# Pre-norm weights applied before the transposes in a hybrid attention block

## The chip, the cores and the metric

The kernel runs on one core of one Trainium2 chip. The metric is the device time of one execution in microseconds; the time shown is the median of three runs, and a further execution was profiled.

## The reference

One layer of a decoder block: x (512 rows of 1024, f32) is RMS-normalised, projected by w_in (1024 x 5912) to the inputs of two attention branches, their gates and their merge gates; the branches are projected, merged, projected by w_o, normalised again and added to x. What the change touches is the first step and the first use of it:

```python
def rms_norm(x, g):
    xf = x.astype(jnp.float32)
    y = xf * lax.rsqrt(jnp.mean(xf * xf, axis=-1, keepdims=True) + RMS_EPS)
    return (y * g.astype(jnp.float32)).astype(x.dtype)
...
    u = rms_norm(x, norm_pre)
    proj = u @ w_in
    q_a, kv_a, g_a, z_a, qkv_b, z_b, merge = jnp.split(proj, splits, axis=-1)
```

## The kernel before, in words

Every product has to be near f32, so an operand is split into a rounded part (hi, type f32r) and the rest (lo), and a product is the sum of hi x hi, lo x hi and hi x lo. The normalised input u is needed transposed (its 1024 columns on the partitions, in eight pieces k, the 512 rows free) and split: the tiles uh and ul, which nearly all that follows reads.

The program has a prologue, then a long stream. The **prologue** (lines 509 to 729) makes uh and ul and, meanwhile, a small projection: 280 columns (values of two NSA branches and the head gates, weights ra, split into wa_hl). The rows come in four tiles tt of 128. For each tile, before:

- x_stats (L554): ACT squares the tile and sums over the row (sq, ss); Vector scales the sum (L514, L564, L565); POOL raises it to -1/2 (L515, L566), which gives rs, one factor a row.
- x_transpose (L581): TensorE, eight blocks of 128 columns, in two halves h. For tiles 0 and 1 the right operand is the diagonal matrix of rs (x_diag, L575), a full f32 product (L588), which scales and transposes at once. For tiles 2 and 3 ACT scales the tile first (x_scale, L579), and the transpose uses the identity (L590).
- x_hi (L593): Vector multiplies the transposed half by the norm_pre weight of each partition (npreT, L596) out of PSUM into SBUF, and ACT rounds it into uh (L600). x_low: the difference goes to ul (L604), on Vector or, for two halves, on POOL.
- a_mm (L618): the small projection, in three parts of eight products: uh by hi weights, ul by hi, uh by lo (parts 0, 1, 2; L626). a_evac_act and a_evac_dve bring the result (pa) into v_slc, v_win and gates.

wa_hi and wa_lo split the small weights, two pieces k a call (ACT L610, POOL L608; lo on Vector or POOL, L613). `first` holds the eight pieces in which the weights of kcvc, the first chunk of the stream, are split (ACT L118, Vector L119). keep_warm (L650) issues products whose result nobody reads. The x and ra loads and the weight loads are all issued on SP's queue, in program order.

What sets the order in the prologue is the program text: inside `with tc.manual_schedule()` each engine's queue takes its instructions in the order in which the lines issue them, and each waits only for its inputs. The exception on POOL are the memsets of rowsel and klos, which are written behind the prologue (L746 to L752) and stand early in POOL's queue all the same; klos is the zero-padded lower part of the keys, first written by the chunk after kcvc.

The **stream** then runs chunk by chunk: each projects uh and ul by a slice of w_in in 512-column products (L171 to L173), while the next chunk's weights are split, and attention units and the merge follow. kcvc's products need all of uh and ul.

Of the kernel before, what the change touches and what calls it, by code (L numbers as in the profile page):

```python
# [41 lines left out]
def hybrid_block(ctx, tc, x, norm_pre, w_in, pe_k, w1_k, w2_k, pe_v, w1_v, w2_v,  # L42
# [469 lines left out]
    def rstd_of(ss, r, eps):  # L512

        dve.tensor_scalar(r, ss, 1.0 / D, eps, op0=ALU.mult, op1=ALU.add)  # L514
        pool.tensor_tensor(r, r, neghalf, op=ALU.pow)  # L515

    warm = const.tile([128, 1], F32, name="warm")
    act.activation(warm, neghalf, AF.Exp)
    xt = [early.tile([128, D], F32, name=f"x_{tt}") for tt in range(NT)]
    npre = early.tile([KT, 128], F32, name="npre")  # L520
    npreT = early.tile([128, KT], F32, name="npreT")
# [15 lines left out]
    nc.sync.dma_start(npre, norm_pre.rearrange("(k p) -> k p", k=KT))  # L537
# [14 lines left out]
    rs, up, sss = {}, {}, {}  # L552

    def x_stats(tt, parts=1):  # L554
        sq = s4.tile([128, D], F32, tag="s4", name=f"sq_{tt}")
        ss = early.tile([128, 2], F32, name=f"ss_{tt}")
        rs[tt] = early.tile([128, 1], F32, name=f"rs_{tt}")
        w = D // parts
        for n in range(parts):
            act.activation(sq[:, n * w:n * w + w], xt[tt][:, n * w:n * w + w], AF.Square, accum_out=ss[:, n:n + 1])  # L560
        sss[tt] = ss
        if parts == 2:
            r = rs[tt]
            dve.tensor_scalar(ss[:, 0:1], ss[:, 0:1], 1.0 / D, EPS, op0=ALU.mult, op1=ALU.add)  # L564
            dve.scalar_tensor_tensor(r, ss[:, 1:2], 1.0 / D, ss[:, 0:1], op0=ALU.mult, op1=ALU.add)  # L565
            pool.tensor_tensor(r, r, neghalf, op=ALU.pow)  # L566

    def x_stats_r(tt):
        rstd_of(sss[tt][:, 0:1], rs[tt], EPS)

    diag = {}

    def x_diag(tt):
        diag[tt] = early.tile([128, 128], F32, name=f"diag_{tt}")
        dve.tensor_scalar(diag[tt], ident, rs[tt], None, op0=ALU.mult)  # L575

    def x_scale(tt, h):
        c = slice(512 * h, 512 * h + 512)
        act.activation(xt[tt][:, c], xt[tt][:, c], AF.Copy, scale=rs[tt])  # L579

    def x_transpose(tt, h):  # L581

        pt = ps("to"[h], f"ut_{tt}_{h}")
        for k in range(4):
            kk = 4 * h + k
            o, i = pt[:, k * 128:(k + 1) * 128], xt[tt][:, kk * 128:(kk + 1) * 128]
            if tt in diag:
                mm(o, i, diag[tt], start=True, stop=True)  # L588
            else:
                pe_eng.transpose(o, i, ident)  # L590
        up[tt, h] = pt

    def x_hi(tt, h):  # L593

# [547 lines left out]
```

## Time and profile before

| | |
|---|---|
| median of the runs shown | 471.07 us (470.97 to 471.8, three runs) |
| the profiled execution | 471.45 us |
| its span, first to last instruction | 469.7 us |
| TensorE (PE) busy | 459.0 us, 98% of the span |
| Vector (DVE) busy | 326.4 us, 69% |
| ACT busy | 255.8 us, 54% |
| POOL (GpSimd) busy | 125.8 us, 27% |
| DMA | 42.08 MB, mean 90 GB/s; 275 GB/s in the first 11.7 us |

Times in the profile count from the first instruction of the span. An engine's busy time says little about what ends last: for that the chain of waits is followed back from the end, and the stretch in question is read instruction by instruction. PE is TensorE's products and PEld its weight loads; a row "x32" merges that many instructions in a row, and "us" of a merged row goes from its start to its end. A full f32 product shows as two rows of PE. A PE row's own duration holds the pipeline; what a stream costs is the spacing of starts.

### The profile page before, as it was taken

What the parts mean: (1) busy time and instruction counts of PE and PEld (TensorE: products, weight loads), DVE (VectorE), ACT (ScalarE), POOL (GpSimd) and SP (SyncE); (2) the same over time, 40 slices, a digit from 0 to 9 for tenths busy, and PEclk for the clock granted to TensorE, in tenths of its full rate; (3) what the DMA queues carried; (4) which work ended last, traced back from release to release, by engine and by line L of the source; (5) the groups of instructions that cost most, each with busy time, mean ns of one, the idle gap of its engine ahead of it and who ended that gap; (6) DMA issues with size and microseconds to landing.
All of it is one profiled execution on the core that took longest, in us unless ns stands there. A gap on an engine that the chain in (4) does not pass through costs nothing.

```text
span 469.7 us, 6991 instructions
## 1 busy us (share of the span) xinstructions
PE 459.0 (98%) x2408; PEld 388.1 (83%) x2408; DVE 326.4 (69%) x837; ACT 255.8 (54%) x684; POOL 125.8 (27%) x144
## 2 busy tenths in 40 slices
PE   7999999999999999999999999999999999999994
PEld 6988887888999888788888888887888888888884
DVE  3858868998777878877798978777674264265044
ACT  5754657776566758656675866675433333234021
POOL 6600006433231333323144443432221010020000
PEclk9999999999999999999999999999999999999998
DMA  8657125023032031130220222132135324224133
GB/s 275 191 161 199 45 51 174 2 77 104 7 84 91 1 91 46 45 89 15 77 91 14 76 89 54 38 92 71 64 93 138 109 63 137 89 89 135 45 134 136
DMA packets 45091, 42.08 MB, mean 90 GB/s; under 512 B 1624, under 2 KB 39808, under 8 KB 45056
## 3 DMA queue, kind: packets, MB, share of 16 engines
q1 hardware_dynamic: 44912, 41.12, 29.4%
q10 hardware_dynamic: 144, 0.52, 0.3%
q8 instruction: 19, 0.31, 0.3%
q14 instruction: 16, 0.13, 0.1%
HBM read 39.54 MB, written 2.10 MB: 89 GB/s over the span
## 4 chain that ended last, share of the span: by engine, by line
PE 88%; DVE 6%; ACT 3%; POOL 1%; issue 1%; POOLq 0%; DVEq 0%; ACTq 0%
PE t L976 5%; PE mm_ga L171 3%; PE mm_ga L172 3%; PE mm_ga L173 3%; PE mm_gb L172 3%; PE mm_gb L173 3%; PE mm_gb L171 3%; PE s L937 3%; PE s L938 3%; PE o L997 3%; PE o L996 3%; PE pa L626 2%; PE mm_qkb L172 2%; PE mm_qkb L173 2%; PE mm_qkb L171 2%; PE mm_vb L290 2%
## 5 line engine op out<-in xcount | busy, mean ns | idle before, releaser
L943 ACT ACTIVATE p<-p,st 128x512 f32<-128x512 f32 (+3 forms) x96 | 53.1, 555 | 23.5 <-DVE st L941 23.2
L955 POOL TENSOR_SCALAR p<-p,st 128x256 f32<-128x256 f32 (+1 forms) x48 | 44.1, 929 | 64.6 <-DVE st L952 22.9
L977 ACT ACTIVATE pt<-t 128x512 fp32r<-128x512 f32 (+1 forms) x72 | 35.4, 524 | 27.4 <-PE t L976 26.8
L978 DVE TENSOR_TENSOR pt<-t,pt 128x512 fp32r<-128x512 f32 (+1 forms) x72 | 40.8, 594 | 8.1 <-ACT pt L977 7.7
L941 DVE CUSTOM_DVE_ANT_0 p<-s,bias_a 128x512 f32<-128x512 f32 (+3 forms) x64 | 29.1, 484 | 10.5 <-PE s L938 10.4
L976 PE MATMUL t<-ident,p 128*128 128x128 f32 x240 | 34.7, 274 | 1.3 <-DVE pt L978 1.0
L976 PEld LDWEIGHTS t<-ident,p 128*128 128x128 f32 x240 | 27.5, 140 | 6.1 <-DVE pt L978 3.3
L354 POOL TENSOR_TENSOR ga<-ga,gb 128x512 f32<-128x512 f32 x8 | 11.7, 1464 | 77.2 <-DVE gb L353 77.2
L1004 POOL TENSOR_TENSOR z<-ot,z 64x512 f32<-64x512 f32 x16 | 20.6, 1285 | 21.8 <-DVE ot L1003 21.8
L171 PE MATMUL mm_qkb<-uh,ws_qkb 128*128 128x512 f32 x64 | 25.8, 404 | 0.0
L171 PE MATMUL mm_gb<-uh,ws_gb 128*128 128x512 f32 x64 | 25.6, 400 | 0.0
L171 PE MATMUL mm_ga<-uh,ws_ga 128*128 128x512 f32 x64 | 25.6, 400 | 0.0
L955 DVE TENSOR_SCALAR p<-p,st 128x512 f32<-128x512 f32 (+1 forms) x48 | 25.2, 564 | 0.5
L172 PE MATMUL mm_gb<-ul,ws_gb 128*128 128x512 f32 x64 | 25.4, 396 | 0.0
L173 PE MATMUL mm_gb<-uh,ws_gb 128*128 128x512 f32 x64 | 25.3, 396 | 0.0
L172 PE MATMUL mm_qkb<-ul,ws_qkb 128*128 128x512 f32 x64 | 25.3, 395 | 0.0
L172 PE MATMUL mm_ga<-ul,ws_ga 128*128 128x512 f32 x64 | 25.3, 395 | 0.0
L173 PE MATMUL mm_ga<-uh,ws_ga 128*128 128x512 f32 x64 | 25.3, 395 | 0.0
L173 PE MATMUL mm_qkb<-uh,ws_qkb 128*128 128x512 f32 x64 | 25.2, 394 | 0.0
L119 DVE TENSOR_TENSOR ws_ab<-raw_ab,ws_ab 128x256 fp32r<-128x256 f32 x32 | 12.8, 455 | 16.7 <-ACT ws_ab L118 16.7
L895 POOL TENSOR_SCALAR bias_a<-dbase 128x512 f32<-128x512 f32 x8 | 13.2, 1650 | 37.8 <-DVE st L941 33.0
L895 POOL TENSOR_SCALAR bias_b<-dbase 128x512 f32<-128x512 f32 x8 | 12.3, 1543 | 38.2 <-DVE st L941 38.2
(312 smaller groups left out, 1388.9 us busy)
## 6 DMA issues: line engine op xcount, KB each, us to landing
raw_qkb<-in_w_in_dram SPq DMA_DIRECT2D x8, 512.0 KB, 5.2
raw_ga<-in_w_in_dram SPq DMA_DIRECT2D x4, 1024.0 KB, 5.1
raw_gb<-in_w_in_dram SPq DMA_DIRECT2D x4, 1024.0 KB, 5.1
raw_wo<-in_w_o_dram SPq DMA_DIRECT2D x4, 1024.0 KB, 5.0
raw_qa<-in_w_in_dram SPq DMA_DIRECT2D x4, 512.0 KB, 6.4
raw_za<-in_w_in_dram SPq DMA_DIRECT2D x4, 512.0 KB, 5.2
raw_vb<-in_w_in_dram SPq DMA_DIRECT2D x2, 1024.0 KB, 5.3
raw_zb<-in_w_in_dram SPq DMA_DIRECT2D x2, 1024.0 KB, 5.6
```

Of the source, the lines that this page charges most:

```text
L171: mm(dst, v[:, 0, k], rh(n), start=(n == 0), stop=False)
L172: mm(dst, v[:, 0, k], rl(n), start=False, stop=False)
L173: mm(dst, v[:, 1, k], rh(n), start=False, stop=(n == len(kts) - 1))
L895: pool.tensor_scalar(t, dbase, slope, None, op0=ALU.mult)
L937: mm(sp[:, 0:nn], q, hi, start=True, stop=False)
L941: dve.tensor_tensor_reduce(pp, src, bias[:, 384 - 128 * i:512], 1.0, 3.0e38, ALU.add, ALU.min, st[:, 0, i:i + 1])
L943: act.activation(pp, pp, AF.Exp, bias=st[:, 0, i:i + 1], scale=-1.0, accum_out=st[:, 1, i:i + 1])
L955: (dve if i >= 2 else pool).tensor_scalar(pp, pp, st[:, 1, i:i + 1], None, op0=ALU.mult)
L976: pe_eng.transpose(tp[:, b * 128:(b + 1) * 128], p_of(u, i)[:, 128 * j:128 * j + 128], ident)
L977: act.activation(h[:, c0:c0 + n], tp[:, 0:n], AF.Copy)
L978: dve.tensor_tensor(l[:, c0:c0 + n], tp[:, 0:n], f(h[:, c0:c0 + n]), op=ALU.subtract)
L1004: pool.tensor_tensor(zs[zt][mine], t[mine], zs[zt][mine], op=ALU.mult)
```

## The change

norm_pre is no longer transposed into one weight a partition. It is loaded as one row (by ACT's queue), and two products with a row of ones (L649) spread it over all 128 partitions into two PSUM tiles npb, one a half. x_scale (L568) multiplies each half tile of x on Vector by rs and by npb in one instruction, in place, for all four tiles; all transposes are then plain ones by the identity (L574); x_hi (L581) rounds straight out of PSUM on ACT, and x_low (L585) reads PSUM too, always on Vector. The 13 warm-ups become 3 ahead of the spreading products and 6 behind them. wa_hi(2) goes to POOL beside wa_hi(4), all wa_lo to Vector. The memsets of rowsel and klos become `clear()`, called near the end of the prologue. The rest of the order is written anew.

```diff
@@ -509,16 +509,13 @@
     early_cm = tc.tile_pool(name="early", bufs=1)
     early = early_cm.__enter__()
 
-    def rstd_of(ss, r, eps):
-
-        dve.tensor_scalar(r, ss, 1.0 / D, eps, op0=ALU.mult, op1=ALU.add)
-        pool.tensor_tensor(r, r, neghalf, op=ALU.pow)
-
     warm = const.tile([128, 1], F32, name="warm")
+    npre = early.tile([1, D], F32, name="npre")
+    nc.scalar.dma_start(npre, norm_pre[None, :])
+    ones = early.tile([1, 128], F32, name="ones")
+    dve.memset(ones, 1.0)
     act.activation(warm, neghalf, AF.Exp)
     xt = [early.tile([128, D], F32, name=f"x_{tt}") for tt in range(NT)]
-    npre = early.tile([KT, 128], F32, name="npre")
-    npreT = early.tile([128, KT], F32, name="npreT")
     ra = early.tile([128, KT, 280], F32, name="ra")
     wa_hl = early.tile([128, 2, KT, 280], F32R, name="wa_hl")
     gates = const.tile([128, NT, 24], F32, name="gates")
@@ -534,7 +531,6 @@
         nc.sync.dma_start(ra[:, k, 128:280], cols(C_VW, 152)[:, k])
 
     load_x(0, 2)
-    nc.sync.dma_start(npre, norm_pre.rearrange("(k p) -> k p", k=KT))
     load_x(1)
     load_ra(0)
     load_ra(1)
@@ -549,59 +545,44 @@
         for i in range(2 if kv == "k" else 1):
             nc.sync.dma_start(t[:, 128 + 64 * i:192 + 64 * i], w2[kv])
 
-    rs, up, sss = {}, {}, {}
+    rs, ut = {}, {}
 
     def x_stats(tt, parts=1):
+
         sq = s4.tile([128, D], F32, tag="s4", name=f"sq_{tt}")
         ss = early.tile([128, 2], F32, name=f"ss_{tt}")
-        rs[tt] = early.tile([128, 1], F32, name=f"rs_{tt}")
+        r = rs[tt] = early.tile([128, 1], F32, name=f"rs_{tt}")
         w = D // parts
         for n in range(parts):
             act.activation(sq[:, n * w:n * w + w], xt[tt][:, n * w:n * w + w], AF.Square, accum_out=ss[:, n:n + 1])
-        sss[tt] = ss
+        part = EPS
         if parts == 2:
-            r = rs[tt]
-            dve.tensor_scalar(ss[:, 0:1], ss[:, 0:1], 1.0 / D, EPS, op0=ALU.mult, op1=ALU.add)
-            dve.scalar_tensor_tensor(r, ss[:, 1:2], 1.0 / D, ss[:, 0:1], op0=ALU.mult, op1=ALU.add)
-            pool.tensor_tensor(r, r, neghalf, op=ALU.pow)
-
-    def x_stats_r(tt):
-        rstd_of(sss[tt][:, 0:1], rs[tt], EPS)
-
-    diag = {}
-
-    def x_diag(tt):
-        diag[tt] = early.tile([128, 128], F32, name=f"diag_{tt}")
-        dve.tensor_scalar(diag[tt], ident, rs[tt], None, op0=ALU.mult)
+            part = ss[:, 0:1]
+            dve.tensor_scalar(part, part, 1.0 / D, EPS, op0=ALU.mult, op1=ALU.add)
+        dve.tensor_scalar(r, ss[:, parts - 1:parts], 1.0 / D, part, op0=ALU.mult, op1=ALU.add)
+        pool.tensor_tensor(r, r, neghalf, op=ALU.pow)
 
     def x_scale(tt, h):
+
         c = slice(512 * h, 512 * h + 512)
-        act.activation(xt[tt][:, c], xt[tt][:, c], AF.Copy, scale=rs[tt])
+        dve.scalar_tensor_tensor(xt[tt][:, c], xt[tt][:, c], rs[tt], npb[h], op0=ALU.mult, op1=ALU.mult)
 
     def x_transpose(tt, h):
-
         pt = ps("to"[h], f"ut_{tt}_{h}")
         for k in range(4):
             kk = 4 * h + k
-            o, i = pt[:, k * 128:(k + 1) * 128], xt[tt][:, kk * 128:(kk + 1) * 128]
-            if tt in diag:
-                mm(o, i, diag[tt], start=True, stop=True)
-            else:
-                pe_eng.transpose(o, i, ident)
-        up[tt, h] = pt
+            pe_eng.transpose(pt[:, k * 128:(k + 1) * 128], xt[tt][:, kk * 128:(kk + 1) * 128], ident)
+        u = pt.rearrange("p (k t) -> p k t", k=4)
+        a = slice(tt * 128, tt * 128 + 128)
+        ut[tt, h] = u, uh[:, 4 * h:4 * h + 4, a], ul[:, 4 * h:4 * h + 4, a]
 
     def x_hi(tt, h):
-
-        u = xt[tt][:, 512 * h:512 * h + 512].rearrange("p (k t) -> p k t", k=4)
-        dve.tensor_tensor(u, up[tt, h].rearrange("p (k t) -> p k t", k=4),
-                          npreT[:, 4 * h:4 * h + 4, None].to_broadcast([128, 4, 128]), op=ALU.mult)
-        hi = uh[:, 4 * h:4 * h + 4, tt * 128:tt * 128 + 128]
-        up[tt, h] = (u, hi)
+        u, hi, lo = ut[tt, h]
         act.activation(hi, u, AF.Copy)
 
-    def x_low(tt, h, eng=dve):
-        u, hi = up[tt, h]
-        eng.tensor_tensor(ul[:, 4 * h:4 * h + 4, tt * 128:tt * 128 + 128], u, f(hi), op=ALU.subtract)
+    def x_low(tt, h):
+        u, hi, lo = ut[tt, h]
+        dve.tensor_tensor(lo, u, f(hi), op=ALU.subtract)
 
     def wa_hi(k, eng=None):
         if eng is not None:
@@ -611,6 +592,16 @@
 
     def wa_lo(k, eng=dve):
         eng.tensor_tensor(wa_hl[:, 1, k:k + 2], ra[:, k:k + 2], f(wa_hl[:, 0, k:k + 2]), op=ALU.subtract)
+
+    def clear():
+
+        pool.memset(rowsel, 0.0)
+        for i in range(4):
+            pool.memset(rowsel[32 * i:32 * i + 32, i % 2:i % 2 + 1], 1.0)
+        for t in klos:
+            for n in range(2):
+                pool.memset(f(t[64:128, n, 0]), 0.0)
+                pool.memset(f(t[0:64, n, 1]), 0.0)
 
     vst["slc"], vst["win"] = s4tile("v_slc"), s4tile("v_win")
     apt = {}
@@ -643,89 +634,97 @@
 
     first = [p for sl in range(2) for p in take_pieces(order[sl])]
     both = (0, 1)
-    wt = ps("mm", "warmup")
+    wt = ps("s", "warmup")
 
     def keep_warm(n):
         for _ in range(n):
             mm(wt, warmup[:, 0:128], warmup[:, 0:512], start=True, stop=True)
 
     with tc.manual_schedule():
-        keep_warm(13)
+        lo, hi = range(0, 4), range(4, 8)
+        keep_warm(3)
+
+        npb = [ps("mm", f"npre_{h}") for h in range(2)]
+        for h in range(2):
+            mm(npb[h], ones, npre[:, 512 * h:512 * h + 512], start=True, stop=True)
+        wt = ps("s", "warmup2")
+        keep_warm(6)
         x_stats(0, 2)
-        pt = ps("t", "npreT_ps")
-        pe_eng.transpose(pt[:, 0:KT], npre, ident[0:KT, 0:KT])
+        x_scale(0, 0)
+        x_transpose(0, 0)
+        x_scale(0, 1)
+        x_hi(0, 0)
+        x_transpose(0, 1)
+        x_low(0, 0)
         x_stats(1)
-        x_diag(0)
-        x_transpose(0, 0)
-        x_stats_r(1)
-        dve.tensor_copy(npreT, pt[:, 0:KT])
+        wa_hi(2, pool)
         wa_hi(0)
-        x_transpose(0, 1)
-        x_diag(1)
+        x_hi(0, 1)
+        a_mm(0, (0,), 2, lo)
+        x_scale(1, 0)
+        a_mm(0, (1,), 2, lo)
+        x_scale(1, 1)
+        x_low(0, 1)
+        wa_hi(4, pool)
         x_transpose(1, 0)
-        wa_hi(2)
-        x_hi(0, 0)
-        wa_hi(4, pool)
         wa_hi(6)
-        wa_lo(4, pool)
         x_transpose(1, 1)
-        x_hi(0, 1)
+        x_hi(1, 0)
+        wa_lo(0)
+        x_hi(1, 1)
+        wa_lo(2)
+        a_mm(0, (0, 1), 2, hi)
         x_stats(2)
-        a_mm(0, (0,))
-        x_hi(1, 0)
-        x_low(0, 0)
-        x_low(0, 1)
-        x_hi(1, 1)
-        x_stats_r(2)
-        a_mm(0, (1,))
-        wa_lo(0)
+        x_low(1, 0)
+        a_mm(0, (2,), 2, lo)
+        x_low(1, 1)
+        a_mm(1, (0,), 2, lo)
+        a_mm(1, (0,), 2, hi)
+        wa_lo(4)
+        a_mm(1, (1,), 2, lo)
+        wa_lo(6)
+        a_mm(1, (1,), 2, hi)
+        x_scale(2, 0)
+        a_mm(1, (2,), 2, lo)
+        x_scale(2, 1)
+        a_mm(0, (2,), 2, hi)
         x_stats(3)
-        a_mm(1, (0,))
-        a_mm(0, (2,), 2, (4, 5, 0, 1))
-        x_scale(2, 0)
-        x_scale(2, 1)
-        wa_lo(2)
-        x_stats_r(3)
-        a_mm(1, (2,), 2, (4, 5, 0, 1))
+        a_evac_act(0)
+        a_mm(1, (2,), 2, hi)
         x_transpose(2, 0)
-        wa_lo(6)
-        x_scale(3, 1)
-        a_mm(0, (2,), 2, (2, 3, 6, 7))
-        x_low(1, 1, pool)
-        x_low(1, 0)
-        x_scale(3, 0)
+        a_evac_dve(0)
         x_transpose(2, 1)
         x_hi(2, 0)
-        a_evac_act(0)
-        a_mm(1, (2,), 1, (2, 3, 6, 7))
+        a_evac_act(1)
+        x_hi(2, 1)
+        a_evac_dve(1)
+        x_low(2, 0)
+        x_scale(3, 0)
+        a_mm(2, (0,), 2, lo)
+        x_scale(3, 1)
+        x_low(2, 1)
+        a_mm(2, (0,), 2, hi)
+        a_mm(2, (2,), 1)
+        x_transpose(3, 0)
         x_transpose(3, 1)
-        x_hi(2, 1)
-        x_low(2, 0)
-        x_low(2, 1, pool)
-        x_transpose(3, 0)
-        a_evac_dve(0)
-        a_mm(1, (1,), 1)
         x_hi(3, 0)
         x_hi(3, 1)
-        a_evac_act(1)
-        a_mm(2, (0,))
+        a_mm(2, (1,), 1)
         x_low(3, 0)
-        a_mm(2, (2,), 1)
-        a_mm(2, (1,), 1)
-        a_evac_dve(1)
+        a_evac_act(2)
         x_low(3, 1)
         first[0]()
-        a_evac_act(2)
         first[1]()
+        a_evac_dve(2)
         first[2]()
         first[3]()
         first[4]()
+        a_mm(3, (0, 2, 1), 1)
         first[5]()
-        a_mm(3, (0, 1, 2))
         first[6]()
+        clear()
         a_evac_act(3)
         a_evac_dve(3)
-        a_evac_dve(2)
         first[7]()
 
     early_cm.__exit__(None, None, None)
@@ -743,13 +742,6 @@
     pool.memset(f(kcs), 0.0)
     pool.memset(f(kcl), 0.0)
     vcs = const.tile([128, 2, 2, 128], F32R, name="vcs")
-    pool.memset(rowsel, 0.0)
-    for i in range(4):
-        pool.memset(rowsel[32 * i:32 * i + 32, i % 2:i % 2 + 1], 1.0)
-    for t in klos:
-        for n in range(2):
-            pool.memset(f(t[64:128, n, 0]), 0.0)
-            pool.memset(f(t[0:64, n, 1]), 0.0)
     blk, pe2, w2t = {}, {}, {}
     for kv in "kv":
         t = cvt[kv]
```

How the queues stand around the first tiles. TensorE, from its start; before:

```order
L650 MATMUL warmup_128<-warmup_79 128x512 x13
L656 MATMUL npreT_ps_152<-ident_78,npre_99 128x8
L588 MATMUL ut_0_0_160<-diag_0_158,x_0_95 128x128 x4
L588 MATMUL ut_0_1_169<-diag_0_158,x_0_95 128x128 x4
L588 MATMUL ut_1_0_176<-diag_1_174,x_1_96 128x128 x4
L588 MATMUL ut_1_1_187<-diag_1_174,x_1_96 128x128 x4
L626 MATMUL pa_0_198<-wa_hl_102,uh_76 128x280 x8
L626 MATMUL pa_0_198<-wa_hl_102,ul_77 128x280 x8
```

and now (warmup, npre and ut are PSUM tiles, ut_0_1 is tile 0, half 1):

```order
L641 MATMUL warmup_129<-warmup_79 128x512 x3
L649 MATMUL npre_0_135<-npre_94,ones_96 128x512
L649 MATMUL npre_1_136<-npre_94,ones_96 128x512
L641 MATMUL warmup2_139<-warmup_79 128x512 x6
L574 MATMUL ut_0_0_155<-ident_78,x_0_99 128x128 x4
L574 MATMUL ut_0_1_162<-ident_78,x_0_99 128x128 x4
L617 MATMUL pa_0_177<-wa_hl_104,uh_76 128x280 x4
L617 MATMUL pa_0_177<-wa_hl_104,ul_77 128x280 x4
L574 MATMUL ut_1_0_190<-ident_78,x_1_100 128x128 x4
L574 MATMUL ut_1_1_196<-ident_78,x_1_100 128x128 x4
L617 MATMUL pa_0_177<-wa_hl_104,uh_76 128x280 x4
```

The diagonal products and npre's transpose are gone; two products from npre stand between the warm-ups, and tile 0's first small products (pa_0) now come ahead of tile 1's transposes.

ACT, from its first square; before:

```order
L560 ACTIVATE sq_0_144,ss_0_145<-x_0_95 128x512 x2
L560 ACTIVATE sq_1_154,ss_1_155<-x_1_96 128x1024
L610 ACTIVATE wa_hl_102<-ra_101 128x560 x2
L600 ACTIVATE uh_76<-x_0_95 128x4x128
L610 ACTIVATE wa_hl_102<-ra_101 128x560
L600 ACTIVATE uh_76<-x_0_95 128x4x128
L560 ACTIVATE sq_2_194,ss_2_195<-x_2_97 128x1024
L600 ACTIVATE uh_76<-x_1_96 128x4x128 x2
```

and now, from the start of its queue:

```order
L514 DMA npre_94<-in_norm_pre_dram 1x1024
L517 ACT_TABLE_LOAD
L517 ACTIVATE warm_93<-neghalf_85 128x1
L557 ACTIVATE sq_0_146,ss_0_147<-x_0_99 128x512 x2
L581 ACTIVATE uh_76<-ut_0_0_155 128x4x128
L557 ACTIVATE sq_1_168,ss_1_169<-x_1_100 128x1024
L591 ACTIVATE wa_hl_104<-ra_103 128x560
L581 ACTIVATE uh_76<-ut_0_1_162 128x4x128
L591 ACTIVATE wa_hl_104<-ra_103 128x560
L581 ACTIVATE uh_76<-ut_1_0_190 128x4x128
L581 ACTIVATE uh_76<-ut_1_1_196 128x4x128
L557 ACTIVATE sq_2_213,ss_2_214<-x_2_101 128x1024
```

x_hi(0,0), the first uh row, moved ahead of tile 1's square; wa_hi's calls on ra stand between x_hi's; tile 2's squares follow both halves of tile 1; the scales of x_2 and x_3 are gone.

Vector, around tile 2's row sum (rs_2 from ss_2); before:

```order
L604 TENSOR_TENSOR ul_77<-x_0_95,uh_76 128x4x128 x2
L596 TENSOR_TENSOR x_1_96<-ut_1_1_187,npreT_100 128x512
L514 TENSOR_SCALAR rs_2_196<-ss_2_195 128x1
L613 TENSOR_TENSOR wa_hl_102<-ra_101,wa_hl_102 128x560 x2
L514 TENSOR_SCALAR rs_3_226<-ss_3_225 128x1
L613 TENSOR_TENSOR wa_hl_102<-ra_101,wa_hl_102 128x560
L604 TENSOR_TENSOR ul_77<-x_1_96,uh_76 128x4x128
L596 TENSOR_TENSOR x_2_97<-ut_2_0_250,npreT_100 128x512
```

and now:

```order
L568 SCALAR_TENSOR_TENSOR x_1_100<-x_1_100,rs_1_170,npre_0_135 128x512
L568 SCALAR_TENSOR_TENSOR x_1_100<-x_1_100,rs_1_170,npre_1_136 128x512
L585 TENSOR_TENSOR ul_77<-ut_0_1_162,uh_76 128x4x128
L594 TENSOR_TENSOR wa_hl_104<-ra_103,wa_hl_104 128x560 x2
L562 TENSOR_SCALAR rs_2_215<-ss_2_214 128x1
L585 TENSOR_TENSOR ul_77<-ut_1_0_190,uh_76 128x4x128
L585 TENSOR_TENSOR ul_77<-ut_1_1_196,uh_76 128x4x128
L594 TENSOR_TENSOR wa_hl_104<-ra_103,wa_hl_104 128x560 x2
L568 SCALAR_TENSOR_TENSOR x_2_101<-x_2_101,rs_2_215,npre_0_135 128x512
L568 SCALAR_TENSOR_TENSOR x_2_101<-x_2_101,rs_2_215,npre_1_136 128x512
```

The sum stood behind all of Vector's work on tile 1 but x_low(1,0), with two wa_lo and tile 3's sum next. Now tile 2's sum stands ahead of x_low for both halves of tile 1 and of the last two wa_lo.

## Rows read from the trace of the kernel before

**Rows 1.** Spans and granted clock of the cores.
```profile
core 0: 469.7 us, clock 0.996
```

**Rows 2.** Stretches (length; busy and count of PE, PEld, DVE, ACT, POOL; clock, DMA, GB/s).
```profile
7.20:10.80 3.60, 3.56 (x32) 3.57 (x32) 2.36 (x6) 2.35 (x6) 0.71 (x2) 1.00 1.10 361
10.80:13.70 2.90, 2.08 (x16) 1.65 (x14) 2.90 (x4) 2.66 (x5) 2.21 (x2) 1.00 1.04 369
13.70:27.00 13.30, 13.30 (x103) 12.86 (x103) 11.43 (x27) 10.80 (x31) 6.21 (x10) 1.00 0.44 116
27.00:470.00 443.00, 435.08 (x2249) 366.43 (x2248) 308.60 (x800) 236.42 (x639) 110.97 (x111) 0.99 0.28 83
```

**Rows 3.** Waits of TensorE from 27 us on (us in total, times, longest).
```profile
PE t L976 <- DVE pt L978: 1.0, 2, 0.6
```

**Rows 4.** Chain of waits, 0 to 28 us (start us, us, what).
```profile
5.82 0.52 POOL klos L752
6.34 0.53 POOL rs L566
...
6.89 0.30 DVE diag L575
...
7.24 2.96 PE ut L588 x24
...
18.74 0.87 PE ut L590 x8
19.61 7.21 PE pa L626 x56
...
27.48 0.23 PE mm_kcvc L172
```

**Rows 5.** Stretches, the warm-up line L650 alone (first: PE busy and count).
```profile
1.50:4.50 3.00, 3.00 (x7) 2.42 (x8) 1.00 0.81 261
```

**Rows 6.** Instructions in order of time, 0 to 7 us.
```profile
0.72 0.86 SPq L529 DMA_DIRECT2D x<-in_x_dram  x2
...
3.45 0.63 ACT L560 ACTIVATE sq<-x 128x512 f32<-128x512 f32 x1 [1.24 <-DMA x<-in_x_dram]
...
4.85 0.16 DVE L565 SCALAR_TENSOR_TENSOR rs<-ss 128x1 f32<-128x1 f32 x1 [0.49 <-ACT sq L560]
...
6.46 1.06 ACT L560 ACTIVATE sq<-x 128x1024 f32<-128x1024 f32 x1 [1.64 <-DMA x<-in_x_dram]
```

**Rows 7.** The tile npost: ACT issue of its load, time to landing.
```profile
L1064 ACTq DMA_DIRECT2D npost<-in_norm_post_dram x1: 379/379/379, 330.3 to 330.3; - x1
...
DMA to landing us min/median/max: 3.7/3.7/3.7
```

**Rows 8.** Groups by line and form, 0 to 27 us.
```profile
L119 DVE TENSOR_TENSOR ws_kcvc<-raw_kcvc,ws_kcvc 128x256 fp32r<-128x256 f32 x7 | 2.5, 418 | 0.7 <-ACT ws_kcvc L118 0.7
...
L751 POOL MEMSET klos<- 64x512 f32 x4 | 2.1, 521 | 0.2
...
L610 ACT ACTIVATE wa_hl<-ra 128x560 fp32r<-128x560 f32 x3 | 1.9, 665 | 1.3 <-DMA ra<-in_w_in_dram 1.3
...
L608 POOL CAST wa_hl<-ra 128x560 fp32r<-128x560 f32 x1 | 0.7, 650 | 2.2 <-DMA ra<-in_w_in_dram 2.2
...
L566 POOL TENSOR_TENSOR rs<-rs,neghalf 128x1 f32<-128x1 f32 x1 | 0.5, 549 | 0.0
```

**Rows 9.** Groups by line and form, whole span.
```profile
L977 ACT ACTIVATE pt<-t 128x512 fp32r<-128x512 f32 x48 | 26.3, 596 | 8.2 <-PE t L976 7.7
...
L353 DVE SCALAR_TENSOR_TENSOR gb<-gb,pb 128x512 f32<-128x512 f32 x8 | 5.5, 687 | 9.5 <-PE pb L173 9.5
```

**Rows 10.** Instructions in order of time, 10 to 18 us.
```profile
10.83 2.81 DVE L604 TENSOR_TENSOR ul<-x,uh 128x512 fp32r<-128x512 f32 x2
...
11.37 1.71 POOL L613 TENSOR_TENSOR wa_hl<-ra,wa_hl 128x560 fp32r<-128x560 f32 x1
...
16.71 0.68 DVE L604 TENSOR_TENSOR ul<-x,uh 128x512 fp32r<-128x512 f32 x1
```

## The prediction

> **What bounds the kernel now.** I read the span and clock first, then the table of stretches, then the waits behind the prologue, then the chain of waits through the prologue, and last the single instructions that the change touches. The span is 469.7 us and the execution took 471.45, so 1.75 us lie around it; TensorE's clock was granted in full but for the tail [rows 1]. From 27.0 us on TensorE is busy 435.1 of 443 us, and its largest wait there is 1.0 us in two pieces [rows 2, 3]. Nothing behind the prologue is touched except the place of some memsets, so the question is one number: when the first product of the chunk kcvc starts. Before, that is 27.0 us (the chain's last row of the prologue, the second kcvc product, stands at 27.48) [rows 4]. Whatever moves that start moves the end by as much.
>
> Inside the prologue the chain runs through the POOL memsets to the power at 6.34, the diagonal at 6.89, and the transposes by it from 7.24 [rows 4]. Then TensorE works 2.08 of 2.90 us between 10.8 and 13.7, and without a gap from 13.7 to 27.0 [rows 2]. TensorE's own work there is dense, so a gain has to come from less of it, or from starting it earlier.
>
> **Work taken off TensorE.** 16 of the 32 transposes were products with the scaled diagonal, full f32, each two rows in the profile: 32 rows kept TensorE 3.56 us, 0.2225 us a product [rows 2]. A plain transpose takes 0.87/8 = 0.109 us [rows 4]. So 16 x 0.1135 = 1.8 us less. The 96 products of the small projection stay at 7.21/56 = 0.129 us each [rows 4].
>
> **Start of the first transposes.** The power for tile 0 no longer stands behind eight klos memsets. Its input is there at 4.85 + 0.16 = 5.01 [rows 6], so it runs about 5.1 to 5.65 (0.55) [rows 8] instead of from 6.31, and x_scale(0,0), 0.69 by the nearest Vector instruction of its form [rows 9], ends at 6.35. Before, the first transpose started at 7.24, so 0.9 us seems to be won. But TensorE's queue holds other work first, in order: three warm-ups, two products that spread norm_pre, six warm-ups. Seven warm-ups are at work in the 3.0 us from 1.5 to 4.5, so 0.43 each at the lower level (1.2 GHz), while 512 columns take 0.23 in the chain's kcvc rows, at the upper level (2.4 GHz) [rows 4, 5]. Three from 1.44, the first a little longer, end near 3.05. npre now comes by ACT's queue; an issue there takes 0.38 us and lands 3.7 us later for 512 KB [rows 7], and 256 KB issued on SP's at 0.72 were used 2.7 us later, at 3.45 [rows 6]. I take 3.4 for the 4 KB, with 2.9 and 4.5 as bounds.
>
> The price of one spreading product (full f32, one row of weights, 512 columns) is not in the trace. The lower bound is two rows at 0.23 = 0.47 us; the upper is the diagonal product scaled by columns, 4 x 0.2225 = 0.89, at the upper level, and twice that at the lower. I take the upper bound, because the diagonal product is the only full-f32 product nearby. The Trainium skill (FP8 and Floating Point Precision, TensorE Precision Notes) says that true fp32 makes four passes through the array; by that, an estimate of 4 x 512/2.4 GHz = 0.85 us, and a sum 0.1 us lower than mine; no row here shows 512 columns.
>
> The first of the two runs at the lower level, 3.4 to 5.2. In the trace before, the warm-ups fall to the short spacing between 4.6 and 4.9 us; if the clock rises about there again, the second takes 0.89, to 6.1, and six warm-ups 1.4, to 7.4. So the transposes start at 7.4, not 6.35, and 0.15 us later than before: the earlier power is hidden under the warm-ups.
>
> **From there to kcvc.** I followed the four queues in their new order, each instruction starting when its engine is free and its inputs are there. TensorE's work from the first transpose is 32 x 0.109 + 96 x 0.129 + 0.2 (two small transposes) = 16.1 us; before it was 3.56 + 16 x 0.109 + 12.4 + 0.2 = 17.9, of the 19.75 from 7.24 to 27.0, so 1.85 us of gaps. The new order has these gaps:
> - ACT takes x_hi(0,0) (0.60 from PSUM [rows 9]) ahead of tile 1's squares. The transposes' result is there at 8.05, the squares follow at 8.55 although x_1 was there at 6.46 [rows 6], and take 1.06 and the accumulator's read; then wa_hi(0), 0.67 [rows 8], which ends at 10.25. TensorE, done with tile 0's transposes at 8.25, waits until 10.3: **2.05 us**.
> - wa_hi(2) stands on POOL behind tile 1's power. The squares are summed at 9.7, the power runs 9.9 to 10.45, the cast (0.65) to 11.1 [rows 8]: TensorE waits another **0.6**.
> - Tile 1's scales end at 11.2 and 11.8, its transposes run 11.95 to 12.8, then products without a gap to 15.4.
> - New wait: Vector's sum of tile 2's squares stands ahead of x_low(1,0), x_low(1,1), wa_lo(4), wa_lo(6) and x_scale(2). ACT does those squares at 13.6 to 14.8, behind x_hi(1,1), so Vector idles 1.2 us and x_low(1,0) ends at 15.55; TensorE waits **0.2**, and 0.1 for x_low(1,1).
> - x_hi(2,0) and x_hi(2,1), with the evacuation of pa_1 between them, cost **0.45 and 0.35** at 19.2 and 20.1.
> - Tile 3 comes in time; TensorE is dense from 20.5.
>
> Together 3.75 us of gaps. 7.4 + 16.1 + 3.75 = 27.25, against 27.0: **0.3 us later**. The same bookkeeping on the old queues gives 26.8 for the 27.0 that the trace shows, so I trust it to 0.2 or 0.3 us, warm-ups apart.
>
> **Edits that cost nothing.** ACT sheds four scales and the other engines gain: Vector exchanges eight weighted evacuations for eight scales, one for one, and takes two x_low and a wa_lo from POOL. The latter were dear: x_low beside POOL's wa_lo took 2.81 us for two, where one alone takes 0.68 [rows 10]. Vector's surplus is covered by TensorE's dense stretch from 12; the rest is in the gaps above. The npre issue moves from SP to ACT ahead of the table load, 0.38 us; ACT first works at 3.45 when x lands [rows 6], so it is covered, and if it were not it would cost 0.38. x_1, ra and the rest leave SP's queue about 0.4 us earlier; tile 1's squares and wa_hi start after their data have landed, so that gains nothing. The klos memsets (eight on two lines, 0.52 each, 4.2 us) [rows 8] run from about 24.8 beside the kcvc weight splits; klos is needed only by the next chunk.
>
> **Against the shown times.** 471.45 + 0.3 = 471.75 for this execution. It lies 0.38 above the median of the runs shown, 471.07, so I predict **471.4 us**. A measurement of this kernel can tell about 0.2% (0.94 us) from no change.
>
> **Rivals.**
> - **The clock rises later** (slower). Before, TensorE worked without a pause for over 3 us before the spacing fell; now there is a pause at 3.05 and one-row products follow. If the level stays low until all nine warm-ups and both products are through, they end at 3.4 + 3.6 + 2.6 = 9.6, 2.2 us after my 7.4, and the time is 473.6; half of it gives 472.5. It decides from a first transpose at about 8.05 on. Against it: both products still keep TensorE at work. The Trainium skill (TensorE: Matmul & The Clock Gate, Part 1) says that the default state is throttled and activity releases it; by that rule the pause could delay the rise, and the trace, with its unbroken warm-ups, doesn't test that. Chance 0.26.
> - **The spreading is cheap.** At 0.47 (0.93 low) a product, npb is whole at 4.8 and the warm-ups end by 6.5. Then everything behind starts 0.9 earlier: kcvc at 26.4, 470.5 us. For it: six warm-ups would then end as x_scale(0,0) does. Chance 0.20.
> - **Faster than my bookkeeping allows.** With the first transpose at 6.4 and the gaps 0.4 us shorter (ACT's squares or POOL's cast a little quicker), kcvc starts at 25.9 and the time is 470.0. Against it: both stand in order behind x_hi(0,0) and the power. Chance 0.12.
> - **The memsets take Vector's way to SBUF.** Vector's x_low went from 0.68 to 1.81 beside a POOL instruction [rows 10]. If memsets beside the weight splits held the first ones (0.42 each [rows 8]) until they end at 29, kcvc's third product would wait 1.6 us: 473.0. Against it: even at 2.6 times their length the splits, four for each of the two slots, outrun TensorE, which takes 1.4 us for the six products of one. Chance 0.04.
> - **My forecast**, between 471.0 and 472.0: 0.38.
>
> **How the numbers follow.** Slower by over 0.2% (above 472.0) is the late clock beyond its first half microsecond, the memsets, and the upper end of npre's landing: 0.30. Faster by over 0.2% (below 470.1) is the third rival and the tail of the second: 0.15. No change that can be told: 0.55. The range leaves out half of the faster rival and the last part of the late clock: 470.1 to 473.4; my forecast's own is 471.0 to 472.0.
>
> **What would show it.** First transpose near 7.4 with x_scale(0,0) done near 6.35 and the six warm-ups between; the second spreading product at half the length of the first; TensorE idle about 2 us before the first small product and 0.6 after its second; Vector idle about 1.2 us ahead of tile 2's sum; kcvc at 27.3. I am wrong if the spreading products end before 5.5 or after 7, or if a change shows in the time that isn't in kcvc's start.

## The result, and the profile of the changed kernel

The changed kernel takes **476.11 us** (median of four, 474.86 to 476.35) against 471.25 in four runs of the kernel before on the same chip: ratio 1.0096, 95% interval 1.0084 to 1.0108. It is slower by 4.9 us, where 471.4 was forecast and the range ended at 473.4. That it is slower is what the rival of the late clock said; the size is beyond even that rival's 473.6.

The span is 4.8 us longer than in [rows 1]:
```profile
core 0: 474.5 us, clock 0.993
```
All but 0.1 us of it lies ahead of kcvc. TensorE's instructions in order of time (start us, us from the first start to the last end, line, output and inputs, partitions x elements, count, then its idle time before them and who ended it):
```profile
1.44 1.65 PE L641 MATMUL warmup<-warmup 128*128 128x512 f32 x3 [1.44 <-DVE warmup L83]
3.02 3.78 PE L649 MATMUL npre<-npre,ones 1*128 1x512 f32 x4
6.72 2.93 PE L641 MATMUL warmup<-warmup 128*128 128x512 f32 x6
9.45 1.39 PE L574 MATMUL ut<-ident,x 128*128 128x128 f32 x8
12.68 0.53 PE L617 MATMUL pa<-wa_hl,uh 128*128 128x280 f32 x2 [1.84 <-ACT wa_hl L591]
13.56 0.83 PE L617 MATMUL pa<-wa_hl,uh 128*128 128x280 f32 x2 [0.35 <-POOL wa_hl L589]
14.19 1.14 PE L617 MATMUL pa<-wa_hl,ul 128*128 128x280 f32 x4
15.12 1.91 PE L574 MATMUL ut<-ident,x 128*128 128x128 f32 x8
...
31.73 0.50 PE L171 MATMUL mm_kcvc<-uh,ws_kcvc 128*128 128x512 f32 x1
```
In the kernel before, eight plain transposes at the full level and the first kcvc product read in the same view:
```profile
18.58 1.03 PE L590 MATMUL ut<-ident,x 128*128 128x128 f32 x8
...
26.97 0.51 PE L171 MATMUL mm_kcvc<-uh,ws_kcvc 128*128 128x512 f32 x1
```
The first kcvc product starts at 31.73 instead of 26.97, and behind it nothing moved: TensorE's busy time is 435.1 us as in [rows 2], and the wait of [rows 3] is the same.
```profile
PE t L968 <- DVE pt L970: 1.0, 2, 0.6
```
Read the spacing of what should be equal. The warm-ups start 2.73/6 = 0.455 us apart from 6.72 to 9.45, where [rows 4] have 0.23: the lower level, 1.2 GHz. The second spreading product is as long as the first (the four rows start at 3.02, 4.03, 4.88 and 5.74), not half as long. Both end at 6.72, inside the 5.5 to 7 that I had named, but for a wrong reason: they began sooner (npre had landed by 3.0) and ran longer. The trace's clock records rise to the full level at 10.16 here, at 4.74 in the kernel before. Then the level falls again. The table of stretches (busy time and count of PE, PEld, DVE, ACT, POOL; granted clock, DMA, GB/s) has one at half clock, which [rows 2] lack:
```profile
13.57:16.99 3.42, 3.42 (x15) 3.41 (x16) 2.66 (x5) 0.70 (x2) 0.53 (x1) 0.50 1.14 311
...
31.73:474.00 442.27, 435.13 (x2249) 366.43 (x2248) 309.08 (x799) 236.92 (x640) 113.68 (x116) 1.00 0.28 83
```
The fall follows TensorE's idle pieces of 1.84 and 0.35 us; behind it TensorE is dense, at half the clock: tile 1's eight transposes take 1.91 us, against the 1.03 above. (The column reads 1.00 also before a trace's first record, so the first microseconds can only be judged by the spacing.)

The idle time sits where the forecast put it. ScalarE's queue shows why TensorE waits for the cast of the weights:
```profile
10.44 0.60 ACT L581 ACTIVATE uh<-ut 128x512 fp32r<-128x512 f32 x1 [4.94 <-PE ut L574]
10.93 1.05 ACT L557 ACTIVATE sq<-x 128x1024 f32<-128x1024 f32 x1
11.88 0.19 ACT L557 ACTIVATION_READ_ACCUMULATOR sq<-x 128x1 f32 x1
11.97 0.66 ACT L591 ACTIVATE wa_hl<-ra 128x560 fp32r<-128x560 f32 x1
```
The squares of tile 1, whose data had landed at 7.1, wait for x_hi(0,0), which waits for the first transposes; the first cast stands behind both.

### The profile page after: what moved, and what is told of

The parts are those of the page before. It is cut to its first block, busy times and chain, and to the rows that moved or that the text cites. A ratio compares the mean times of both kernels' runs of the same rounds, so it can differ in the third digit from the quotient of the medians.

```text
span 474.5 us, 6949 instructions
## 1 busy us (share of the span) xinstructions
PE 463.0 (98%) x2391; PEld 388.7 (82%) x2391; DVE 326.8 (69%) x838; ACT 252.7 (53%) x679; POOL 121.3 (26%) x142
## 4 chain that ended last, share of the span: by engine, by line
PE 89%; DVE 4%; ACT 3%; issue 2%; DMA 1%; POOL 0%; POOLq 0%; DVEq 0%; SPq 0%; ACTq 0%
PE t L968 5%; PE mm_ga L171 3%; PE mm_ga L173 3%; PE mm_ga L172 3%; PE s L929 3%; PE mm_gb L172 3%; PE mm_gb L173 3%; PE s L930 3%; PE mm_gb L171 3%; PE pa L617 3%; PE mm_qkb L172 3%; PE o L989 3%; PE mm_qkb L173 3%; PE mm_qkb L171 3%; PE o L988 3%
```

## Experiments

I split the 4.8 us of kcvc in three before testing: the first transposes start 2.2 us later (9.45 against 7.24); what follows runs partly at the lower level; and the new order may cost something of itself. **Theory:** products with one row of weights (one partition) leave TensorE at its lower level, and that is nearly all. **Rivals:** full-f32 products of any shape do it; the memsets or the order do it.

**1 and 2. The kernel before with two idle products, of one row and of 128.** No other change; nothing reads the products.
```
-        keep_warm(13)
+        keep_warm(3)
+        dry = [ps("s", f"dry_{h}") for h in range(2)]
+        for h in range(2):
+            mm(dry[h], f(warmup[0:1, 0:128]), f(warmup[0:1, 0:512]), start=True, stop=True)
             # 0:128 in the second
+        keep_warm(6)
```


> The old kernel with its 13 warm-ups replaced by 3, two full-f32 products of 512 columns with one row of weights (their result is read by nobody), and 6 more; the rest untouched. Theory (the one-row products leave TensorE's clock at its lower level): both products take 1.7 us, the six warm-ups 0.43 each, the first transposes start at 8.9 to 9.4 instead of 7.24 and run slow at first, kcvc starts 1.7 to 4 us later: 473 to 475.5 us. Rival (the new order of the queues costs the time, the clock is as before): the second product already runs at the upper level, all is done by 6.9, before the diagonal is there at 7.2: 471.2, within 0.4.

> The same as e1 but with 128 rows of weights in the two products instead of one. Theory (one row is the cause): the clock rises as in the kernel before, near 4.7 us, all is done by 7.0, no change: 471.2, within 0.4. Rival (any full-f32 product, or their length, leaves the clock low): as e1, 473 to 475.5.

One row: 473.35 us, ratio 1.0046 (1.0031 to 1.0061). 128 rows: 471.24, ratio 1.0002 (0.9993 to 1.0011). TensorE in order of time, one row first:
```profile
3.02 3.78 PE L656 MATMUL dry<-warmup 1*128 1x512 f32 x4
6.73 2.93 PE L650 MATMUL warmup<-warmup 128*128 128x512 f32 x6
9.59 0.27 PE L660 MATMUL npreT_ps<-ident,npre 8*128 8x8 f32 x1
9.79 1.40 PE L588 MATMUL ut<-diag,x 128*128 128x128 f32 x7
...
28.37 0.50 PE L171 MATMUL mm_kcvc<-uh,ws_kcvc 128*128 128x512 f32 x1
```
and 128 rows:
```profile
2.88 3.35 PE L656 MATMUL dry<-warmup 128*128 128x512 f32 x4
5.51 2.09 PE L650 MATMUL warmup<-warmup 128*128 128x512 f32 x6
7.54 0.22 PE L660 MATMUL npreT_ps<-ident,npre 8*128 8x8 f32 x1
7.69 3.50 PE L588 MATMUL ut<-diag,x 128*128 128x128 f32 x29
...
27.12 0.50 PE L171 MATMUL mm_kcvc<-uh,ws_kcvc 128*128 128x512 f32 x1
```
The same products, columns and place: with one row the clock rises at 10.56, with 128 at 5.83. TensorE counts as busy in both, so busy time alone didn't tell. The first rival falls. Of the first run's expectation the time held (473 to 475.5), but the first transposes came at 9.79, later than the 8.9 to 9.4 expected, and kcvc 28.37 - 26.97 = 1.40 us later in the profiled execution (472.82, the fastest of the four), less than the 1.7 to 4.

**3. The kernel before with only the memsets moved.**
```
+        clear()            # rowsel and klos memsets, behind first[6]() instead of ahead of the powers
```


> The old kernel with the one part of the change that moves the memsets of rowsel and klos behind the powers, to the same place as in the change. Theory: tile 0's power runs at 5.1 instead of 6.3, the first transposes start at about 6.2 instead of 7.24; tile 1's power keeps its time, so part of the gain is lost: kcvc 0.3 to 0.9 us earlier, 470.4 to 470.9 us. Rival (memsets beside Vector's weight splits hold these up): no gain or a loss, 471.2 to 473.

471.26, ratio 1.0001 (0.9992 to 1.001), where 470.4 to 470.9 was expected. The first transposes do start a microsecond earlier, and the second tile's don't, because tile 1's squares wait for its load:
```profile
6.20 2.05 PE L588 MATMUL ut<-diag,x 128*128 128x128 f32 x16
9.16 2.05 PE L588 MATMUL ut<-diag,x 128*128 128x128 f32 x16 [0.90 <-DVE diag L575]
```
VectorE's weight splits now run beside the memsets of klos, and take what they took without them. The kernel before, then this run:
```profile
24.63 2.10 DVE L119 TENSOR_TENSOR ws_kcvc<-raw_kcvc,ws_kcvc 128x256 fp32r<-128x256 f32 x6 [0.68 <-ACT ws_kcvc L118]
```
```profile
24.52 2.11 DVE L119 TENSOR_TENSOR ws_kcvc<-raw_kcvc,ws_kcvc 128x256 fp32r<-128x256 f32 x6 [0.69 <-ACT ws_kcvc L118]
...
25.11 0.53 POOL L622 MEMSET klos<- 64x512 f32 x1
```
The memsets cost nothing, and bring nothing.

**4. The changed kernel with nine warm-ups in TensorE's idle time** behind tile 0's transposes.
```
         x_transpose(0, 1)
+        keep_warm(9)
```


> The changed kernel with nine more warm-ups behind tile 0's transposes, where TensorE sat idle for 1.8 us (10.8 to 12.7) before the clock fell to the lower level from 13.6 to 17.0. Theory (that idle stretch lets the clock fall): the clock stays up, the 3.4 us at half rate shrink to 1.7, kcvc starts near 30.1 instead of 31.7: 474.3 to 474.8 us. Rival (the order alone sets the time, the clock is a side effect): 476 or a little later.

474.99, ratio 1.0079 (1.0062 to 1.0096): 1.1 us less than the changed kernel, a little over the 474.3 to 474.8 expected, and kcvc starts at 30.82, not near 30.1.
```profile
9.45 1.91 PE L574 MATMUL ut<-ident,x 128*128 128x128 f32 x8
11.01 3.15 PE L641 MATMUL warmup<-warmup 128*128 128x512 f32 x9
...
15.04 1.03 PE L574 MATMUL ut<-ident,x 128*128 128x128 f32 x8
```
The clock rises at 12.79, later than the 10.16 of the changed kernel, so tile 0's transposes are slow too (1.91 us against 1.39); from then on it stays up, and tile 1's take 1.03. The 1.1 us are what the filling brings in all; run 4 alone doesn't price the fall. The changed kernel's own runs agree with a price of that order: its mean granted clock was 0.993 or 0.994 in the three that took 476.03 to 476.35, and 0.996 in the one that took 474.86, and a stretch of 3.4 us at half the clock takes about 0.004 off that mean.

**5 to 7. Three cures tried at once.** 128 rows in the spreading products; or nine warm-ups ahead of the one-row products; or the latter with nine more in the idle time.
```
-    npre = early.tile([1, D], F32, name="npre")                 # 5: 32 rows loaded, 96 of zeros,
-    nc.scalar.dma_start(npre, norm_pre[None, :])                #    weights 1/32
+    npre = early.tile([128, D], F32, name="npre")
+    nc.scalar.dma_start(npre[0:32], norm_pre[None, :].to_broadcast([32, D]))
...
-        keep_warm(3)                                            # 6 and 7, and none behind
+        keep_warm(9)
```


> The changed kernel, in which only the two spreading products change: their weights have 128 rows (32 of them 1/32 of the sum each on a row of weights that is loaded 32 times, 96 on zeros), the same 512 columns in the same place behind three warm-ups. Theory (one row of weights in the products is what keeps TensorE at its lower level, and all of the loss hangs on the clock): the clock record is full from about 6, as in the old kernel with full-row products (5.83), the first transposes stand at 7.4 to 7.9, the kcvc products begin at 27.3 to 27.9, and the time is 471.3 to 472.0, my forecast of 471.4 within its error. If the 2 us idle of TensorE behind the first transposes drops the clock again, as it did in the changed kernel (which cost 1.1 us there), 472.4 to 473.1. Rival (the new order costs several us of itself, whatever the clock): 474 or more, with the clock up early.

> The changed kernel with nine warm-ups ahead of the two spreading products (still one row of weights) and none behind them. The clock should rise at about 4.8 as in the old kernel, from the warm-ups alone, and the products run at the upper level, near 1.9 us for both, ending near 7. Theory A (one-row products only don't lift the clock; one that is up stays up for their 1.9 us): first transposes 7.4 to 7.7, kcvc at 27.3 to 27.9, 471.3 to 472.0. Theory B (one-row products count as idleness, so that the clock falls behind them): half clock over the first transposes and beyond, kcvc 29 or later, 473 or more. The rival of an order that costs several us of itself gives 474 or more under a clock that stays up.

> The same with nine further warm-ups in the 2 us in which TensorE waits behind the transposes of tile 0. If the clock falls in that idle time in the kernel without them, this one is faster by the price of that fall, about 1 us; if it doesn't fall there, the two agree to 0.5 us. Theory A: 471.0 to 471.9. Rival of a costly order: 474 or more.

474.6 (ratio 1.0072), 474.4 (1.0068) and 473.78 (1.0055, 1.004 to 1.007). None came to the 471 to 472 of a cured clock, and by the times alone the rival of a costly order would have won in the first two. The traces say otherwise; in none was the clock up through the stage. In 5 the load of 32 rows landed at 4.2, so the products came after a pause and the warm-ups were again slow:
```profile
4.33 3.75 PE L651 MATMUL npre<-npre,ones 128*128 128x512 f32 x4 [1.25 <-DMA npre<-in_norm_pre_dram]
7.10 3.00 PE L643 MATMUL warmup<-warmup 128*128 128x512 f32 x6
9.93 1.03 PE L576 MATMUL ut<-ident,x 128*128 128x128 f32 x8
12.81 0.53 PE L619 MATMUL pa<-wa_hl,uh 128*128 128x280 f32 x2 [1.84 <-ACT wa_hl L593]
...
30.36 0.50 PE L171 MATMUL mm_kcvc<-uh,ws_kcvc 128*128 128x512 f32 x1
```
In 6 the nine warm-ups do lift the clock (at 5.83), the one-row products follow from 5.58 to 7.71, and it falls at 9.25 for almost 7 us:
```profile
9.30:16.10 6.80, 5.42 (x22) 5.07 (x23) 3.88 (x7) 4.01 (x8) 1.76 (x3) 0.50 1.06 357
```
In 7 it falls at 8.71 though TensorE is dense, and the filling warm-ups run low:
```profile
5.47 1.98 PE L649 MATMUL npre<-npre,ones 1*128 1x512 f32 x4
7.50 1.55 PE L574 MATMUL ut<-ident,x 128*128 128x128 f32 x8
8.71 3.89 PE L641 MATMUL warmup<-warmup 128*128 128x512 f32 x9
```
So theory B of the sixth run holds: a clock that is up falls behind one-row products. From the fifth comes a price for the order: the clock is full from 9.31 there, and kcvc starts 30.36 - 9.93 = 20.43 us behind the first transposes, where the kernel before has 26.97 - 7.24 = 19.73.

**8 and 9. 128 rows behind nine warm-ups, without and with the filling.** One row over a tile of zeros, weights all one.
```
+    dve.memset(npre, 0.0)              # [128, D]
+    dve.memset(ones, 1.0)              # [128, 128]
     act.activation(warm, neghalf, AF.Exp)
+    nc.scalar.dma_start(npre[0:1], norm_pre[None, :])
```


> The changed kernel with nine warm-ups ahead of the spreading products, none behind them, and 128 rows in the products (the row of norm weights over a tile of zeros, weights all one; the load of the row is issued behind ScalarE's first exponential and should land near 4.6, before the ninth warm-up ends). Theory (products on one row count as no work for the clock, wherever they stand; full rows do): clock full from 4.8 on, products at the upper level for 1.8 us, first transposes at 7.4 to 7.7. With 20.4 us from there to the first kcvc product, as the kernel with full rows and a late clock had it (9.93 to 30.36), kcvc begins at 27.8 to 28.1 and the time is 471.9 to 472.3: what the new order costs by itself, 0.8 to 1.2 us more than before. If the clock falls in the idle 2 us of TensorE, a microsecond more, 472.9 to 473.5. Rival (one row against 128 makes no difference, only the place of the products does): the same as the kernel with nine warm-ups first and one row, 474.4, with a clock that falls at 9 to 10.

> The same with nine more warm-ups in TensorE's 2 us behind the transposes of tile 0: 471.9 to 472.3 by the theory, clock full from 4.8 to the tail; equal to the kernel without them if the clock doesn't fall there. Rival (one row or 128 alike): 473.8, as the filled kernel with one row.

474.59 (ratio 1.0067, 1.0049 to 1.0085) and 473.09 (1.005, 1.0031 to 1.0068): both over their expectation, because the row, issued late behind the x loads, landed at 7.1 and 6.1 and not at 4.6. The ninth stays at the full level to the tail:
```profile
6.09 1.97 PE L650 MATMUL npre<-npre,ones 128*128 128x512 f32 x4 [0.44 <-DMA npre<-in_norm_pre_dram]
8.10 1.45 PE L575 MATMUL ut<-ident,x 128*128 128x128 f32 x8
9.31 2.33 PE L642 MATMUL warmup<-warmup 128*128 128x512 f32 x9
...
28.61 0.50 PE L171 MATMUL mm_kcvc<-uh,ws_kcvc 128*128 128x512 f32 x1
```
Against the seventh, with the same TensorE queue, the rows differ and the products start 0.6 us later, behind 0.44 us of waiting; the nine filling warm-ups take 2.33 us instead of 3.89. The mean granted clock was 0.993 or 0.994 in all four runs of the seventh and 0.996 to 0.999 in the eight of the ninth. One of those eight took 476.36 us, which no trace explains. Tile 0's plain transposes stand behind the products in both, so the rows decide between the two; whether transposes weigh on the clock as well is not shown. The eighth fell to half from 13.18 to 16.59, behind its two idle pieces of 1.49 and 0.34 us; the fifth, with 1.84 and 0.35, did not fall. A fall thus can follow such idle time and need not. The ninth again has 28.61 - 8.10 = 20.51 us from the first transposes to kcvc.

**10 and 11. An early spreading, with the change's order and with another.** The row is loaded as 128 x 8 and put on a diagonal by VectorE; the products follow six warm-ups.
```
+    nc.scalar.dma_start(npre, norm_pre.rearrange("(p k) -> p k", k=KT))
+    for h in range(2):
+        q = slice(64 * h, 64 * h + 64)
+        dve.tensor_tensor(nd[:, q], ident[:, q, None].to_broadcast([128, 64, KT]),
+                          npre[:, None, :].to_broadcast([128, 64, KT]), op=ALU.mult)
...
+        rest1 = x_stats(1) # 11 only: its squares ahead of x_hi(0, 0)
...
         x_transpose(0, 1)
+        keep_warm(7)       # and tile 1's transposes right behind
...
+        x_transpose(1, 0)
```


> The changed kernel and its order with the spreading cured: the row weights are loaded early as 128 x 8, VectorE spreads them on a diagonal (two products with the identity, about 0.6 us each, while it waits for the squares), and the two products with ones on 128 rows stand behind six warm-ups from about 4.1; nine warm-ups fill TensorE's wait behind the transposes of tile 0. Theory (the clock costs 4 of the 4.9 us; what is left is the new order, 20.5 us from the first transposes to kcvc where the kernel before had 19.7): clock full from about 4.9, products ended by 6.0, first transposes at 6.8 to 7.2, kcvc at 27.2 to 27.7, 471.3 to 471.9. Rival (the order costs more than that, or the early first transposes are lost again at tile 1, whose load sets its squares, as they were in the kernel before with its memsets late): 20.9 us or more from the first transposes, 472.2 or later.

> The same spreading, and another order of the stage: squares of tile 1 ahead of the first cast on ScalarE, tile 1 transposed right behind tile 0 with seven warm-ups between, the low parts and evacuations put where a queue model made from the durations of this trace has the fewest waits. By that model kcvc begins at 25.9; it put the order of the change 0.5 us too early, so 26.2 to 26.6 here against 27.0 of the kernel before: 470.3 to 470.8. If TensorE's real wait is set by the loads (tile 1, then the weights), which no order moves, the gain is gone and it stands at 471.2 or above.

The tenth takes 472.42 (ratio 1.0024, 1.0015 to 1.0033), the eleventh **470.73** (0.9993, 0.9984 to 1.0002), in ten and eleven runs. The tenth's time, 3.7 us below that of the changed kernel, is that of the rival, its trace that of the theory: the products began after a short pause at 4.50, the clock rose at 6.54, and the first transposes stand at 7.47, 0.3 to 0.7 late; but from there to kcvc it is 27.99 - 7.47 = 20.52 us once more, not 20.9. So the order costs about 0.75 us when the transposes start this early.
```profile
4.50 2.98 PE L654 MATMUL npre<-nd,ones 128*128 128x512 f32 x4
7.47 0.66 PE L579 MATMUL ut<-ident,x 128*128 128x128 f32 x4
...
27.99 0.50 PE L171 MATMUL mm_kcvc<-uh,ws_kcvc 128*128 128x512 f32 x1
```
The eleventh has warm-ups in its one long wait, and all but the first kcvc product start at 26.23 or later, within the 26.2 to 26.6 expected:
```profile
6.99 1.45 PE L584 MATMUL ut<-ident,x 128*128 128x128 f32 x8
8.20 1.87 PE L651 MATMUL warmup<-warmup 128*128 128x512 f32 x7
9.98 0.66 PE L584 MATMUL ut<-ident,x 128*128 128x128 f32 x4
...
26.23 0.50 PE L172 MATMUL mm_kcvc<-ul,ws_kcvc 128*128 128x512 f32 x1
```
It takes 1.1% less than the changed kernel (470.73 against 476.11); against the kernel before, 0.4 us less, its interval just reaches 1, so I don't claim that gain.

## Why the prediction was wrong

**The step that failed** is in the start of the first transposes: "if the clock rises about there again, the second takes 0.89, to 6.1, and six warm-ups 1.4, to 7.4". It didn't rise there. By the trace: npre 3.02 (3.4 assumed), both products 3.70 us (1.8 + 0.89), six warm-ups 2.73 (1.4): 9.45, not 7.4. The product's price itself was good at its level: its two rows start 0.85 us apart at the lower, 1.71 us a product against 2 x 0.89, and 0.43 apart at the upper in the ninth run, 0.86 against 0.89. The Trainium skill (FP8 and Floating Point Precision, TensorE Precision Notes) has true fp32 in four passes, from which 0.85 was estimated. The ninth run's 0.86 agrees. What failed is the premise that TensorE at work on the products is enough to lift the clock: with one row of weights it wasn't (runs 1 and 2).

**The rival of the late clock** had the mechanism and the place, 9.6 for the first transposes. Two things were wrong in it. Its argument against itself, "both products still keep TensorE at work", was the error; it named the pause and the one row, and I gave it 0.26. And it let everything behind 9.6 run at the full level: 473.6. Instead kcvc started 31.73 - 9.45 = 22.28 us behind the first transposes, where a full clock gives 20.5 (runs 5, 9, 10): **1.8 us** more of clock, 1.1 of which came back by filling the idle time (run 4). I had counted the 2 us of idleness as 2 us, not as something the clock could answer.

The Trainium skill (TensorE: Matmul & The Clock Gate, Part 1) says that the default state is throttled and activity releases it. The traces agree with the default and the release (4.74 in the kernel before), but show that a busy TensorE is not always activity in that sense: with 3.78 us of one-row products among the warm-ups the clock rose at 10.56 (run 1), and behind 1.98 us of them it fell at 8.71 (run 7).

**The sum, as measured:** first transposes + 2.2 us, clock behind them + 1.8, order + 0.75 (about 20.5 against 19.73): kcvc's 4.76, and 4.86 in the times. The 1.8 is what the other two leave, so the sum closes by itself, and it isn't the only split. The old order can swallow part of a delay: in the profiled execution of run 1 its first transposes came 2.55 us later and kcvc only 1.40, its gaps all but closed (18.58 us from one to the other). The new order took 20.43 to 20.52 us at a full clock whether it began at 7.47 or at 9.93, so there a delay counts in full. What needs no split is run 10: with the clock mended and the idle time filled, the same order takes 472.42 us instead of 476.11.

**What held, and what was off, step by step:**
- That only kcvc's start moves: yes, 4.76 of 4.86 us.
- 16 x 0.1135 us off the transposes: eight plain ones take 1.03 us at the full level in this order too (run 4), so the price held, and the gaps ate the gain, as forecast.
- Gaps of 2.05 and 0.6: measured 1.84 and 0.35, by the causes named. VectorE's wait ahead of tile 2's sum was forecast at 1.2 and is 2.50 us, where runs 5, 9 and 10 with a full clock have 1.00:
```profile
18.73 0.15 DVE L562 TENSOR_SCALAR rs<-ss 128x1 f32<-128x1 f32 x1 [2.50 <-ACT sq L557]
```
- From the first transposes to kcvc 19.85 us were forecast and 20.5 measured at a full clock: 0.6 us short, two to three times the 0.2 to 0.3 that I trusted the bookkeeping to.
- x_scale(0,0) was forecast to end at 6.35. The power ran at 5.90, not 5.1, as the second half of x_0 landed at 4.75 (4.08 before). It didn't matter; the warm-ups ended 2 us later still.
- "The memsets take Vector's way to SBUF" (0.04) is refuted by run 3: 2.11 us against 2.10.
- "The spreading is cheap" (0.20) is refuted by the product's price, 0.86 us at the upper level and not 0.47; "faster than my bookkeeping" (0.12) needed an early rise that did not come. Even with the clock mended, the change's order gave no time below 471.85 (run 10).

## What to carry to other kernels

Ahead of a stage that TensorE bounds, look at a small product's partitions before its length: one on a single row occupies the engine and leaves it at, or lets it back to, the lower level (only one row and 128 were tried here, nothing between). Spread the row over 128 partitions first, or spread elsewhere, and check the spacing of the next equal matmuls. When a forecast has TensorE idle for microseconds soon after its clock rose, price a fall too, or fill the gap with warm-ups, and try the filling alone. And when a cure misses its time, read whether the cure took hold before giving the time to the rival: runs 5 to 9 missed for the most part through late loads or the clock.

## Unexpected of the hardware

- Two full-f32 products of 512 columns on one row, 3.78 us, delayed the rise of the clock from 5.83 to 10.56; on 128 rows they cost nothing (471.24 against 473.35 us). A tile of which all rows but one are zeros held the level too (run 9).
- The rise itself wanders: with the same nine warm-ups from 1.44 it came at 5.30 in run 7, at 5.83 in run 6, at 6.12 in run 9 and at 6.35 in run 8.
- The load of one 4 KB row was used 2.3 us after its issue at 0.7, but 3.6 and 4.6 us after an issue at 2.5, with four loads issued ahead of it on SP's queue (runs 9 and 8); TensorE waited for it there. That these loads held it up is argued, not tested. Beside a load of 32 rows at 0.7 the first half of x_0 landed at 4.44 instead of 3.36 (run 5).
